# Recurrent stage of a hybrid block: reversed value tiles moved through DRAM one by one, and the heads' steps filled otherwise

## The chip, the cores and the metric

The kernel runs on one core of a Trainium2 chip. A core has a matrix engine (PE in the profile; its weight loads are PEld), VectorE (DVE), ScalarE (ACT), GpSimd (POOL) and a queue engine, SyncE (SP). Each engine works through its own instructions in order. Transfers are issued by SP, ACT or POOL and run on 16 DMA engines that all queues share. The metric is the device time of one execution in microseconds (us), the median of several runs.

## The reference

One transformer-like block on 1024 tokens of width 1024, in float32. `h` is the normalised input; `h @ w_in` gives nine projections. Three parts follow:

```python
o_hg = hgrn2_mixer(hq, hf, hi, lower_bounds[layer])      # recurrent: 8 heads, 128 keys, 128 values
o_hg = rms_norm(o_hg, hg_out_norm[layer]).reshape(b, s, HG_WIDTH) * jax.nn.sigmoid(hg)
o_sb = stick_breaking(q, k, v)                            # attention: 16 heads of 64
mixed = jax.nn.sigmoid(ga) * (o_hg @ w_hg_out) + jax.nn.sigmoid(gb) * (o_sb @ w_sb_out)
x = x + mixed @ w_o
x = x + (jax.nn.silu(gate) * up) @ w_ffn_out              # gate, up from rms_norm(x) @ w_ffn_in
```

The recurrent mixer is the part that the change touches. Its state is a 128 x 128 matrix for each head, worked out chunk by chunk (64 tokens):

```python
def step(state, inp):
    q_c, k_c, v_c, g_c = inp
    cum = jnp.cumsum(g_c, axis=-2)
    decay = jnp.exp(jnp.where(causal, cum[:, :, :, None, :] - cum[:, :, None, :, :], -jnp.inf))
    scores = jnp.einsum('bhtd,bhtsd,bhsd->bhts', q_c, decay, k_c)
    o = (jnp.einsum('bhts,bhsv->bhtv', scores, v_c)
         + jnp.einsum('bhtd,bhdv->bhtv', q_c * jnp.exp(cum), state))
    last = cum[:, :, -1:, :]
    state = (jnp.exp(last[:, :, 0, :, None]) * state
             + jnp.einsum('bhsd,bhsv->bhdv', k_c * jnp.exp(last - cum), v_c))
    return state, o
```

`q_c`, `k_c` and `g_c` come from the projections `hq` and `hf`, and the values `v_c` from the projection `hi`.

## The kernel before, in words

Every product of float32 operands is made from three matmuls (`mm3`, lines 229 to 233): each operand is split into a rounded part and a remainder (`wh`, `wl` for weights). `load_w` (from line 128) loads a block of weights with SP (`wr`), rounds it with ACT, and has POOL subtract it by an accumulating DMA (`rest_by_dma`, lines 123 to 126). Two `wr` buffers and three of `wh` and `wl` go round.

The program runs in stages: the projections of the first heads (`Pairs`, a scheme that saves products and needs sums of the quarters of `h`, the list `h_sums`), the recurrent stage, the attention stage, the output products and the feed-forward part.

In the recurrent stage the loop `for h in range(NH)` at the end of the quoted code runs over eight heads. A head has `prep` (decayed keys and queries, by POOL, ACT and DVE) and fifteen steps, the list at the end of `hg_head`: `base(0)`, `base(1)`, `across`, `level(0)` to `level(3)` (scores of pairs of ever smaller stretches, gathered in `sc`), `turn` (transposes of decayed keys, copied by ACT to `ket`, line 658), `state` (products of keys and values, line 667, joined to states by DVE), `read` (the outputs, lines 715 and 717) and `norm`. Each step works on tiles of 128 tokens; the eight tiles come in pairs `tp` = 0 to 3, the second of each pair with its tokens in reversed order.

The values `v` of heads h and h+1 come from one projection (`hg_v`, `proj_v`), four pairs of tiles for two heads together. The first tile of each pair is copied from PSUM into `v` by ACT (line 560). The second has to be reversed over the partitions, and that goes through DRAM: ACT copies it to `vs` (line 557), SP stores it to `d_v` (line 558), a DRAM-to-DRAM transfer on ACT's queue (`turn_v`, line 564) writes the rows of all four to `d_vr` in reversed order, and two transfers on ACT's queue (`load_v`, line 568) bring them to `v[:, 1::2]`. `turn_v(h)` stands at the start of `prep` of the even head h; for head 0 after its values; `load_v(h)` with `base(0)`. `state(0)` needs tiles 0 to 3 of `v`, `state(1)` tiles 4 to 6, `read(1)` also tile 7.

PE's order is exactly that of the program. `weave(own, fill, lead)` writes it: between a head's own steps it puts `fill`, other work for PE, in proportion to the numbers that the list gives each step, after `lead` units at the start. The fill of head h is the query projection of the next head (`hg_q`, 16 steps of 0.65, called q steps here), then `hg_gates` of the next head (0.0), and then half of the values of the next pair of heads (`hg_v`, 32 steps of 0.33, v steps): tiles 0 and 1 in the even heads, 2 and 3 in the odd ones. Heads 6 and 7 have gate projections in place of values. Loads, copies and other engines' instructions are ordered by a planner: it goes by the order of the program as priority and its own estimate of when each instruction can start, so one that is ready early can be put ahead of one that was written before it. Once the order is fixed, each engine and queue keeps it.

Of the kernel before, what the change touches and what calls it, by code (L numbers as in the profile page):

```python
# [16 lines left out]
P = 128  # L17
# [24 lines left out]
def hybrid_block(ctx, tc, x, norm1_gain, w_in, lb_logits, hg_out_norm, sb_q_norm, sb_k_norm,  # L42
                 w_hg_out, w_sb_out, w_o, norm2_gain, w_ffn_in, w_ffn_out,
                 c_ident, c_blk, c_lvl, c_base, out):
    nc = tc.nc
# [69 lines left out]
    d_v, d_vr = (dp.tile([NH // 2, NT // 2, P, 2 * P], F32, name=n) for n in ("d_v", "d_vr"))  # L115
# [293 lines left out]
    hd = [dict() for _ in range(NH)]  # L409
# [139 lines left out]
    def hg_v(h, tiles=range(4), get=None):  # L549
        get = get or in_block(2048 + h * P, 256)  # L550

        def evac(tp, ps):
            if tp == 0:
                for j in range(2):
                    hd[h + j]["v"] = hg.tile([P, NT, P], F32, tag="v", bufs=4, name="v")
            vs = hg.tile([P, 2 * P], F32, tag="vs", name="vs")
            nc.scalar.copy(vs, ps[:, 2 * P:])
            nc.sync.dma_start(d_v[h // 2, tp], vs)
            for j in range(2):
                nc.scalar.copy(hd[h + j]["v"][:, 2 * tp, :], ps[:, j * P:(j + 1) * P])  # L560
        return proj_v(get, evac, tiles)

    def turn_v(h):
        nc.scalar.dma_start(d_vr[h // 2], d_v[h // 2, :, ::-1, :])

    def load_v(h):
        for j in range(2):
            nc.scalar.dma_start(hd[h + j]["v"][:, 1::2, :],
                                d_vr[h // 2, :, :, j * P:(j + 1) * P].rearrange("a p c -> p a c"))

    def hg_load(h):
        d = hd[h]
# [17 lines left out]
    def hg_head(h):  # L590
        d = hd[h]
        sg, q, v, kv, c = (d[n] for n in ("sg", "q", "v", "kv", "c"))
# [2 lines left out]

        def prep():
            if h % 2 == 0 and h > 0:
                turn_v(h)
            sc = e["sc"] = hg.tile([P, S], F32, tag="sc", bufs=1, name="sc")
            nc.gpsimd.memset(sc, 0.0)  # L600
            kb = e["kb"] = hg.tile([P, S], F32, tag="kl", bufs=4, name="kb")
            qb = e["qb"] = hg.tile([P, S], F32, tag="kl", bufs=4, name="qb")
            c4 = c.rearrange("p (b l) -> p b l", l=4)
            nc.gpsimd.tensor_sub(qb.rearrange("p (b l) -> p b l", l=4), c4,
                                 c4[:, :, 1:2].broadcast_to([P, S // 4, 4]))
            for dst, src in by_tile(kb, qb):
                nc.scalar.activation(dst, src, AF.Exp, scale=-1.0)
            nc.scalar.activation(qb, qb, AF.Exp)
            order(nc.vector.tensor_mul(kb, kb, kv), *last.get("own", ()))
            nc.vector.tensor_mul(qb, qb, q)  # L610
            ke = e["ke"] = hg.tile([P, S], F32, tag="ke", bufs=1, name="ke")
            for dst, src in by_tile(ke, c):
                dst, src = (a.rearrange("p a (n c) -> p a n c", c=CH) for a in (dst, src))
                nc.gpsimd.tensor_sub(dst, src[:, :, :, CH - 1:CH].broadcast_to([P, NT // 2, 2, CH]), src)
            nc.scalar.activation(ke, ke, AF.Exp)
            order(nc.vector.tensor_mul(ke, ke, kv), *last.get("own", ()))
            el = e["el"] = hg.tile([P, 64], F32, tag="el", name="el")[:, 0:NCH]
            nc.scalar.activation(el, c3[:, :, CH - 1], AF.Exp)
            qe = e["qe"] = hg.tile([P, S], F32, tag="qe", bufs=1, name="qe")
            nc.scalar.activation(qe, c, AF.Exp)  # L620
            nc.vector.tensor_mul(qe, qe, q)

        def base(g):
            kb, qb = e["kb"], e["qb"]
            ps = pbank("pz")
            for j in range(4):
                t = 4 * g + j
                nc.tensor.matmul(ps[:, j * P:(j + 1) * P], kb[:, t * P:(t + 1) * P],
                                 qb[:, t * P:(t + 1) * P], start=True, stop=True)
            nc.vector.copy_predicated(e["sc"][:, g * HS:(g + 1) * HS], bmask, ps)  # L630

        def across():
            ke, qe, el = e["ke"], e["qe"], e["el"]
            ps = pbank("pz")
            for t in range(NT):
                r0 = t % 2 * CH
                nc.tensor.matmul(ps[r0:r0 + CH, t * CH:(t + 1) * CH], ke[:, t * P + r0:t * P + r0 + CH],
                                 qe[:, t * P + CH:(t + 1) * P], start=True, stop=True)
            for w, rows in enumerate((slice(0, CH), slice(CH, P))):
                nc.scalar.copy(pairs(e["sc"])[rows, :, w, CH:], ps[rows, :].rearrange(  # L640
                    "p (a two c) -> p a two c", two=2, c=CH)[:, :, w, :])
            el2 = el.rearrange("p (t two) -> p t two", two=2)
            nc.vector.tensor_mul(chunk0(ke), chunk0(ke), el2[:, :, 1:2].rearrange("p (a two) o -> p a two o", two=2)
                                 .broadcast_to([P, NT // 2, 2, CH]))
            nc.vector.tensor_mul(bl(qe, CH)[:, :, 1, :], bl(qe, CH)[:, :, 1, :],
                                 el2[:, :, 0:1].broadcast_to([P, NT, CH]))
            eb = e["eb"] = hg.tile([P, 64], F32, tag="eb", name="eb")[:, 0:NT]
            nc.vector.tensor_mul(eb, el2[:, :, 0], el2[:, :, 1])
# [28 lines left out]
        def level_prep(li):  # L677
            L = LEVELS[li]
            kq = hg.tile([P, 2, HS], F32, tag="kl", bufs=4, name="kq")
            kp, qr = kq[:, 0, :], kq[:, 1, :].rearrange("p (b l) -> p b l", l=L)  # L680
            halves = [a.rearrange("p a (b two l) -> p a b two l", two=2, l=L)[:, :, :, 0, :]
                      for k3 in [kp.rearrange("p (a x) -> p a x", x=P)] for a in (k3, odd(k3))]
            cl = bl(c, L)
            for w, dst in enumerate(halves):
                src = pairs(c)[:, :, w, :].rearrange("p a (b two l) -> p a b two l", two=2, l=L)[:, :, :, 0, :]
                nc.vector.tensor_sub(dst, src[:, :, :, L - 1:L].broadcast_to([P, NT // 2, P // (2 * L), L]), src)
            nc.gpsimd.tensor_sub(qr, cl[:, :, 1, :], cl[:, :, 0, L - 1:L].broadcast_to([P, HS // L, L]))
            nc.scalar.activation(kq, kq, AF.Exp)
            nc.vector.tensor_mul(qr, qr, bl(q, L)[:, :, 1, :])
            k4 = kp.rearrange("p (a b two l) -> p a b two l", two=2, l=L, a=NT // 2)  # L690
            for w in range(2):
                nc.vector.tensor_mul(k4[:, :, :, w, :], k4[:, :, :, w, :], pairs(kv)[:, :, w, :].rearrange(
                    "p a (b two l) -> p a b two l", two=2, l=L)[:, :, :, w, :])
            e[li] = kq
# [27 lines left out]
        def norm(half):  # L722
# [7 lines left out]
            nc.sync.dma_start(d_ohg[h][:, sl], r)  # L730

        return prep, [
            (0.86, lambda: (base(0), load_v(h) if h % 2 == 0 else None, level_prep(0),)),
            (2.46, lambda: (base(1), level_prep(1),)),
            (5.60, lambda: (across(), level_prep(2),)),
            (2.24, lambda: (level(0), level_prep(3),)),
            (0.50, lambda: (turn(0),)),
            (0.80, lambda: (turn(1),)),
            (0.85, lambda: (level(1),)),
            (1.85, lambda: (state(0),)),  # L740
            (0.70, lambda: (state(1),)),
            (0.61, lambda: (level(2),)),
            (3.99, lambda: (level(3),)),
            (1.60, lambda: (read(0),)),
            (4.50, lambda: (read(1),)),
            (2.97, lambda: (norm(0),)),
            (0.45, lambda: (norm(1),)),
# [54 lines left out]
    for n in range(n0):  # L802
        if n == n0 - 5:
            get = in_block(2048, 256)
            get()
            v0 = [hg_v(0, tiles, get) for tiles in ((0, 1), (2, 3))]
        weave([], pairs0.steps(n))
        if h_sums:
            h_sums.pop(0)()
    s0ctx.close()  # L810
    hg = hgctx.enter_context(tc.tile_pool(name="hg", bufs=2, reuse_waits="tile"))
# [4 lines left out]
    prep, own = hg_head(0)  # L816
    prep()
    weave([], v0[1])
    turn_v(0)
    def urgent(steps):  # L820
        def run(f):
            with tc.high_priority():
# [3 lines left out]
    for h in range(NH):  # L826
        if h < NH - 1:
            fill = hg_q(h + 1) + [(0.0, lambda: hg_gates(h + 1))]
            if h == NH - 2:
                fill += gate_steps(1)  # L830
            if h < NH - 2:
                fill += hg_v(h + 1, (2, 3)) if h % 2 else hg_v(h + 2, (0, 1))
        else:
            fill = gate_steps(2)
        load_blocks()
        if h > 0:
            prep, own = hg_head(h)
            prep()
        if h < NH - 1:
            hg_load(h + 1)  # L840
        weave(own, fill, lead=5.53)
    hgctx.close()


# [686 lines left out]
```

## Time and profile before

| | |
|---|---|
| median of 3 runs | 2054.48 us (2050.78 to 2055.08) |
| the profiled execution | 2053.37 us; span from first to last instruction 2051.3 us |
| PE, DVE, ACT, POOL busy | 98%, 74%, 56%, 16% of the span |
| mean granted PE clock | 0.993 |
| `d_vr<-d_v` (ACT queue) | 4 issues of 512 KB |
| `v<-d_vr` (ACT queue) | 8 issues of 256 KB, 2.8 us to landing |
| `d_v<-vs` (SP queue) | 16 issues of 128 KB, 1.7 us to landing |

How to read it: a row of a group or a timeline names the line of the kernel, the engine, the operation, `out<-in` by the names of the program, the shape and the count; square brackets hold the idle time of the engine just before it and what ended it. A row of waits reads "engine, tile, line <- who released it: us in total, times, longest". A busy PE is not PE at its peak, since matmuls overlap and a low clock makes them longer.

### The profile page before, as it was taken

The numbers are of one execution on the slowest core, as the hardware profiler recorded it, in microseconds if no ns is written. First come the engines' busy times: TensorE is split into PE (matmuls) and PEld (weight loads), VectorE is DVE, ScalarE is ACT, GpSimd is POOL, SyncE is SP. The second block draws the span as 40 slices with busy tenths as digits, with TensorE's granted clock in tenths as the row PEclk, the third lists the DMA queues.
The fourth block names the chain that finished last, engine by engine and source line by source line (L and its number), as shares of the span: only waits on it lengthen the run. The fifth ranks groups of instructions, "written<-read, shape, count | busy, mean of one in ns | idle before, by whom it ended". The sixth has DMA issues, their size and how long they took to land.

```text
span 2051.3 us, 29673 instructions
## 1 busy us (share of the span) xinstructions
PE 2006.9 (98%) x10963; PEld 1720.6 (84%) x10963; DVE 1522.5 (74%) x2355; ACT 1141.7 (56%) x1957; POOL 318.4 (16%) x431
## 2 busy tenths in 40 slices
PE   8999899999999999999999999998999999999999
PEld 8888788898888988988988888887888888888887
DVE  7853777787367877787787598999766666668975
ACT  7544464555377777777777465547433333334443
POOL 0000444444222332332231000000000000000000
PEclk9999999999999999999999999999999999999999
DMA  5234446545455445455445646413323222256131
GB/s 184 98 114 144 128 120 158 144 114 152 117 117 125 89 107 118 99 118 121 101 105 120 216 147 210 166 35 111 102 74 105 78 72 77 78 203 222 42 113 41
DMA packets 209840, 245.23 MB, mean 120 GB/s; under 512 B 12008, under 2 KB 142496, under 8 KB 209696
## 3 DMA queue, kind: packets, MB, share of 16 engines
q1 hardware_dynamic: 188928, 202.84, 31.4%
q0 software_dynamic: 13616, 35.14, 10.3%
q10 hardware_dynamic: 7152, 5.37, 0.8%
q8 instruction: 86, 1.41, 0.3%
q14 instruction: 58, 0.48, 0.1%
HBM read 146.57 MB, written 51.12 MB: 96 GB/s over the span
## 4 chain that ended last, share of the span: by engine, by line
PE 71%; DVE 9%; DMA 4%; issue 2%; ACT 2%; POOL 1%; DVEq 0%; POOLq 0%; ACTq 0%
PE pd L231 14%; PE pd L232 14%; PE pd L233 14%; DMA d_vr<-d_v 3%; PE pt L1011 3%; PE pt L233 3%; PE pt L231 3%; PE pt L232 3%; PE po L1028 2%; PE po L231 2%; PE po L1027 2%; PE po L232 2%; PE po L233 2%; PE pz L966 2%; PE pz L967 2%
## 5 line engine op out<-in xcount | busy, mean ns | idle before, releaser
L167 ACT CAST wh<-u 128x512 fp32r<-128x512 f32 (+1 forms) x280 | 183.5, 684 | 224.9 <-PE po L233 86.6
L231 PE MATMUL pd<-hT,wh 128*128 128x512 f32 (+1 forms) x716 | 286.7, 400 | 0.0
L232 PE MATMUL pd<-hT,wh 128*128 128x512 f32 (+1 forms) x716 | 276.0, 385 | 0.5 <-DVE hT L281 0.5
L233 PE MATMUL pd<-hT,wl 128*128 128x512 f32 (+1 forms) x688 | 264.9, 385 | 0.0
L231 PE MATMUL pd<-u,wh 128*128 128x512 f32 x496 | 194.0, 391 | 1.5 <-ACT c L1394 0.7
L232 PE MATMUL pd<-u,wh 128*128 128x512 f32 x496 | 193.1, 389 | 0.2 <-DVE u L168 0.2
L168 DVE TENSOR_TENSOR wl<-u,wh 128x512 fp32r<-128x512 f32 (+1 forms) x196 | 150.5, 801 | 45.7 <-ACT wh L167 43.6
L231 PE MATMUL pd<-wh,hT 128*128 128x256 f32 x512 | 153.6, 300 | 0.0
L233 PEld LDWEIGHTS pd<-hT,wl 128*128 128x128 f32 x688 | 129.2, 188 | 26.9
L978 DVE TENSOR_TENSOR_SCAN kp<-kp,dsel 128x512 f32<-128x512 f32 (+3 forms) x128 | 123.5, 965 | 37.0 <-ACT kp L971 36.4
L232 PEld LDWEIGHTS pd<-hT,wh 128*128 128x128 f32 x716 | 135.2, 189 | 18.7 <-DVE hT L281 0.9
L231 PEld LDWEIGHTS pd<-hT,wh 128*128 128x128 f32 x716 | 135.0, 189 | 18.2
L232 PE MATMUL pd<-wl,hT 128*128 128x256 f32 x512 | 145.7, 285 | 2.7 <-DMA wl<-wr 1.7
L233 PE MATMUL pd<-wh,hT 128*128 128x256 f32 x512 | 145.6, 284 | 0.0
L971 ACT ACTIVATE kp<-pz,rq 128x128 f32<-128x128 f32 (+2 forms) x192 | 114.2, 595 | 43.9 <-PE pz L967 33.2
L233 PE MATMUL pd<-u,wh 128*128 128x512 f32 x352 | 137.0, 389 | 0.0
L164 DVE TENSOR_TENSOR u<-u,u 128x512 f32<-128x512 f32 (+1 forms) x152 | 124.7, 855 | 12.3 <-DMA u<-d_ohg 7.6
L1014 DVE TENSOR_TENSOR tl<-pt,th 128x512 fp32r<-128x512 f32 (+1 forms) x160 | 100.2, 627 | 33.5 <-ACT th L1013 33.1
L985 DVE TENSOR_TENSOR a<-a,kp 128x128 f32<-128x128 f32 (+2 forms) x192 | 109.7, 571 | 17.8 <-ACT a L971 3.4
L971 ACT ACTIVATE a<-pz,rq 128x128 f32<-128x128 f32 (+2 forms) x192 | 114.3, 595 | 7.0 <-PE pt L1011 7.0
L231 PEld LDWEIGHTS pd<-u,wh 128*128 128x128 f32 x496 | 93.1, 188 | 21.6 <-ACT c L1394 1.1
L232 PEld LDWEIGHTS pd<-u,wh 128*128 128x128 f32 x496 | 93.1, 188 | 19.8 <-DVE u L168 0.5
(305 smaller groups left out, 5293.5 us busy)
## 6 DMA issues: line engine op xcount, KB each, us to landing
wr<-in_w_in SPq DMA_DIRECT2D x72, 512.0 KB, 4.0
wl<-wr POOLq DMA_DIRECT2D x59, 512.0 KB, 4.9
u<-in_w_ffn_in SPq DMA_DIRECT2D x24, 512.0 KB, 4.7
wr<-in_w_ffn_in SPq DMA_DIRECT2D x20, 512.0 KB, 4.2
u<-in_w_ffn_out SPq DMA_DIRECT2D x10, 1024.0 KB, 6.7
d_act<-c SPq DMA_DIRECT2D x33, 256.0 KB, 2.1
u<-d_act SPq DMA_DIRECT2D x8, 1024.0 KB, 5.7
qh<-qh SPq DMA_DIRECT2D x48, 128.0 KB, 2.4
```

Source lines behind the costliest of these rows:

```text
L164: e.tensor_tensor(raw(to), raw(a), raw(b), op=op)
L167: nc.scalar.copy(hi, src)
L168: e.tensor_sub(lo, src, hi.bitcast(F32))
L231: nc.tensor.matmul(ps, lh, rh, start=start, stop=False, skip_group_check=adds)
L232: nc.tensor.matmul(ps, lh, rl, start=False, stop=False, skip_group_check=adds)
L233: nc.tensor.matmul(ps, ll, rh, start=False, stop=stop, skip_group_check=adds)
L966: nc.tensor.matmul(ps[:, :n], qhi[:, qs], kk[:, k0:k0 + n], start=True, stop=False)
L971: last["sig"] = [nc.scalar.activation(t[:, 0:w], ps[:, 0:w], AF.Sigmoid, scale=rq[:, n_, col:col + 1]) for n_, t in enumerate((kp, a))]
L978: nc.vector.tensor_tensor_scan(rev, rev, dsel[:, HS - w:][:, ::-1], initial=0.0, op0=ALU.mult, op1=ALU.max)
L985: nc.vector.tensor_mul(a[:, 0:w], a[:, 0:w], kp[:, 1:w + 1])
L1011: nc.tensor.transpose(tp[:, s * P:(s + 1) * P], a[:, b * P:(b + 1) * P], ident)
L1014: nc.vector.tensor_sub(tl[:, c0:], tp[:, c0:], th[:, c0:].bitcast(F32))
```

## The change

- `turn_v(h, tp)` now moves one tile of a pair of heads: 128 rows in reversed order, each as two runs of 128 numbers, with the two heads as the outer dimension. It is issued by ACT. Tiles 0 to 2 are moved after the store of the tile behind them (`tp > 0` in `evac`), tile 3 with the step `base(1)` of the even head.
- `load_v(h, tiles)` is issued by SP: tiles 0 to 2 at the start of `prep` of the even head (for head 0 after its values), tile 3 with `level(1)`.
- The numbers of the steps for `weave` are others, and `lead` is 3.64 instead of 5.53.
- In the first stage the remaining `h_sums` begin after the third step of `pairs0` instead of the first.

```diff
@@ hg_v, evac
             nc.sync.dma_start(d_v[h // 2, tp], vs)
+            if tp > 0:
+                turn_v(h, tp - 1)
@@
-    def turn_v(h):
-        nc.scalar.dma_start(d_vr[h // 2], d_v[h // 2, :, ::-1, :])
-
-    def load_v(h):
+    def turn_v(h, tp):
+        dst, src = (d[h // 2, tp].rearrange("p (j c) -> j p c", j=2) for d in (d_vr, d_v))
+        nc.scalar.dma_start(dst, src[:, ::-1, :])
+
+    def load_v(h, tiles):
         for j in range(2):
-            nc.scalar.dma_start(hd[h + j]["v"][:, 1::2, :],
-                                d_vr[h // 2, :, :, j * P:(j + 1) * P].rearrange("a p c -> p a c"))
+            nc.sync.dma_start(hd[h + j]["v"][:, 1 + 2 * tiles.start:2 * tiles.stop:2, :],
+                                d_vr[h // 2, tiles, :, j * P:(j + 1) * P].rearrange("a p c -> p a c"))
@@ prep
             if h % 2 == 0 and h > 0:
-                turn_v(h)
+                load_v(h, slice(0, 3))
@@ hg_head, the list of steps
-            (0.86, lambda: (base(0), load_v(h) if h % 2 == 0 else None, level_prep(0),)),
-            (2.46, lambda: (base(1), level_prep(1),)),
-            (5.60, lambda: (across(), level_prep(2),)),
+            (1.53, lambda: (base(0), level_prep(0))),
+            (2.70, lambda: (base(1), turn_v(h, 3) if h % 2 == 0 else None, level_prep(1),)),
+            (3.27, lambda: (across(), level_prep(2),)),
             (2.24, lambda: (level(0), level_prep(3),)),
-            (0.50, lambda: (turn(0),)),
-            (0.80, lambda: (turn(1),)),
-            (0.85, lambda: (level(1),)),
-            (1.85, lambda: (state(0),)),
-            (0.70, lambda: (state(1),)),
+            (0.35, lambda: (turn(0),)),
+            (0.49, lambda: (turn(1),)),
+            (0.85, lambda: (level(1), load_v(h, slice(3, 4)) if h % 2 == 0 else None,)),
+            (1.79, lambda: (state(0),)),
+            (0.60, lambda: (state(1),)),
             (0.61, lambda: (level(2),)),
-            (3.99, lambda: (level(3),)),
-            (1.60, lambda: (read(0),)),
+            (11.14, lambda: (level(3),)),
+            (0.47, lambda: (read(0),)),
             (4.50, lambda: (read(1),)),
             (2.97, lambda: (norm(0),)),
             (0.45, lambda: (norm(1),)),
@@ first stage
-        if h_sums:
+        if h_sums and n > 1:
             h_sums.pop(0)()
@@ before the loop over the heads
-    turn_v(0)
+    load_v(0, slice(0, 3))
@@ the loop
-        weave(own, fill, lead=5.53)
+        weave(own, fill, lead=3.64)
```

## The prediction, made before the result was known

> **What bounds the kernel now.** I read the page first (span and busy time), then the busy time by stretch, one stretch for each head of the recurrent stage, then what the matrix engine (PE) waited for, and last the chain of waits and the DMA queues round those waits.
>
> ```profile
> span 2051.3 us, 29673 instructions
> ...
> PE 2006.9 (98%) x10963; PEld 1720.6 (84%) x10963; DVE 1522.5 (74%) x2355; ACT 1141.7 (56%) x1957; POOL 318.4 (16%) x431
> ```
>
> PE sets the end nearly everywhere, so an edit pays only where PE idles or runs slowly. The stretches below are heads 0 to 4 (start and end of a head are where its first fill step runs). The columns are stretch, length, then busy time and count of PE, PEld, DVE, ACT, POOL, the granted PE clock, the DMA share and GB/s.
>
> ```profile
> 217.90:266.50 48.60, 38.34 (x266) 34.93 (x265) 34.68 (x52) 23.20 (x36) 13.51 (x14) 0.89 0.45 117
> 266.50:303.50 37.00, 35.94 (x265) 32.82 (x264) 28.86 (x51) 22.13 (x36) 18.71 (x15) 1.00 0.53 136
> 303.50:345.70 42.20, 37.81 (x266) 34.43 (x265) 31.28 (x45) 22.59 (x37) 16.38 (x15) 0.96 0.53 144
> 345.70:382.50 36.80, 35.74 (x264) 32.63 (x263) 28.62 (x50) 21.89 (x35) 18.67 (x15) 1.00 0.53 136
> 382.50:426.00 43.50, 39.16 (x265) 35.80 (x264) 31.24 (x45) 22.54 (x37) 16.36 (x15) 0.92 0.51 140
> ```
>
> Odd heads take 37 us, even ones 42 to 49, with the same PE instructions. Two things differ: idle time, and PE busy time at a lower clock (35.84 on average in heads 1 and 3 against 38.34, 37.81 and 39.16, so 2.50 + 1.97 + 3.32 = 7.8 us lost to the clock). The idle time of the whole stage (195 to 560 us), by cause:
>
> ```profile
> PE pt L667 <- ACT ket L658: 13.8, 5, 8.4
> PE pt L667 <- DMA v<-d_vr: 3.3, 4, 1.0
> PE pt L715 <- DVE sc L703: 2.5, 3, 1.1
> PE pd L232 <- DMA wl<-wr: 1.7, 2, 0.9
> PE pz L390 <- DVE sql L385: 1.3, 3, 0.4
> PE pd L232 <- ACT kq L688: 1.0, 1, 1.0
> ```
>
> The first two groups are the `state(0)` matmuls of the even heads, in the timeline of PE:
>
> ```profile
> 246.28 0.80 PE L667 MATMUL pt<-v,ket 128*128 128x128 f32 x2 [8.39 <-ACT ket L658]
> 247.54 0.80 PE L667 MATMUL pt<-v,ket 128*128 128x128 f32 x2 [0.46 <-DMA v<-d_vr]
> ...
> 325.39 0.49 PE L667 MATMUL pt<-v,ket 128*128 128x128 f32 x2 [2.07 <-ACT ket L658]
> 326.89 1.65 PE L667 MATMUL pt<-v,ket 128*128 128x128 f32 x6 [1.01 <-DMA v<-d_vr]
> ...
> 404.39 0.49 PE L667 MATMUL pt<-v,ket 128*128 128x128 f32 x2 [2.13 <-ACT ket L658]
> 405.85 1.44 PE L667 MATMUL pt<-v,ket 128*128 128x128 f32 x5 [0.98 <-DMA v<-d_vr]
> ...
> 481.84 0.49 PE L667 MATMUL pt<-v,ket 128*128 128x128 f32 x2 [0.63 <-ACT ket L658]
> 483.14 0.94 PE L667 MATMUL pt<-v,ket 128*128 128x128 f32 x6 [0.81 <-DMA v<-d_vr]
> ```
>
> That is 8.85 + 3.08 + 3.11 + 1.44 = 16.5 us. The chain of waits of head 2 and ScalarE's timeline there say why:
>
> ```profile
> 303.74 0.26 ACT vs L557
> ...
> 305.81 17.95 DMA d_vr<-d_v
> ...
> 323.78 3.07 DMA v<-d_vr
> ```
> ```profile
> 324.75 0.97 ACT L658 COPY ket<-pt 128x512 f32<-128x512 f32 x2 [7.48 <-DMA d_vr<-d_v]
> ```
>
> The turn through DRAM begins when the last of four tiles has been stored, takes 17.95 us, and its loads (3.07 us) stand in ScalarE's own queue: ScalarE idles 7.48 us in front of them, and its next copy, `ket`, feeds the same matmuls.
>
> **The tile moves and loads.** The rows of the DMA queues: the turn of head 2 and then its loads (share of 16 engines in stretches of 17.9 and 3.5 us), the store of one tile, the weight remainders that run beside the turn, and SP's queue.
>
> ```profile
> q10 hardware_dynamic: 516, 0.52, 9.0%
> wl<-wr POOLq DMA_DIRECT2D x2, 512.0 KB, 11.6
> ```
> ```profile
> q10 hardware_dynamic: 1056, 0.52, 51.6%
> ```
> ```profile
> d_v<-vs SPq DMA_DIRECT2D x16, 128.0 KB, 1.7
> ```
> ```profile
> 217.57 0.32 SPq L558 DMA_DIRECT2D d_v<-vs  x1
> ...
> 290.07 0.37 SPq L136 DMA_DIRECT2D wr<-in_w_in  x1
> 292.25 12.12 SPq L558 DMA_DIRECT2D d_v<-vs  x2
> 305.99 2.97 SPq L730 DMA_DIRECT2D d_ohg<-r  x2
> 309.01 0.77 SPq L575 DMA_DIRECT2D sg<-d_g  x1
> 317.04 4.51 SPq L136 DMA_DIRECT2D wr<-in_w_in  x2
> ```
>
> The old turn is 512 packets of 1 KB and 4 more; 9.0% of 16 engines over 17.9 us is 25.8 us, 50 ns a packet. I read the 4 as one completion per engine used: 128 packets on each of four engines, 6.4 us of work stretched to 17.95 by the other queues. The loads come out the same way at 27 ns a packet of 512 B, on all 16 engines.
>
> The new move of one tile is 256 packets of 512 B. No row shows it. Its lower bound is the 128 KB store, 1.7 us; its upper bound the whole old turn, 17.95. I take 8: 128 packets at 50 ns on each of two engines, 6.4, and 1.7 to begin and land.
>
> The Trainium skill (DMA: Bandwidth & Descriptors, section "Why a DMA increments its semaphore by 16 and not by 1") says that a copy runs on the largest number of engines up to 16 that divides the outermost dimension of both sides; the 4 extra packets of the old turn, with four tiles outermost, agree. By it the new form, with the two halves outermost, gets two engines, which speaks against the change.
>
> When is the third tile, the last that `state` needs, in place? Its source is stored at 292.25 (the first of the two), landed 1.7 later. Queue orders come from the planner, which lets a ready transfer pass: the weights that PE uses from 303.5 on were issued by 290.07, though the program names them at head 2. So the move should be issued between 294.0 and, if it stays behind the copy `vs` of tile 3, 304.0. With 8 for the move and 3.07 for the load, `v` lands between 305.1 and 315.1.
>
> When does PE want it? The fill list of an even head is 16 q steps (0.65 each) and 32 v steps (0.33), 20.96. `weave` pumps it to lead + (20.96 - lead) x done/sum. After `level(1)` that was 5.53 + 15.43 x 13.31/29.98 = 12.38 (16 q, 7 v) and becomes 3.64 + 17.32 x 11.43/33.96 = 9.47 (15 q). Two PE rows of head 2 price a step, and two more rows set head 0 and the `h_sums` edit:
>
> ```profile
> 313.53 0.69 PE L637 MATMUL pz<-qe,ke 128*64 128x64 f32 x16
> 317.00 1.05 PE L702 MATMUL pz<-kq 128*128 128x128 f32 x8
> ```
> ```profile
> 227.17 0.36 ACT L557 COPY vs<-pd 128x256 f32<-128x256 f32 x1
> ```
> ```profile
> 76.77 0.50 PE L231 MATMUL pd<-hi,wh 128*128 128x512 f32 x1 [1.21 <-ACT c L516]
> ```
>
> Four q steps lie between the first two: (317.00 - 313.53 - 0.69)/4 = 0.70 us each; a v step has half the columns, 0.35. So `state(0)` comes 0.70 + 7 x 0.35 = 3.2 us earlier. In head 2 it was due at 325.39 - 2.07 = 323.3, of which 0.9 was the wait for `wl` before it; it will be due at 319.2. The loads have landed 4 to 14 us before. Heads 4 and 6 repeat this, so heads 2, 4 and 6 lose 3.08 + 3.11 + 1.44 us of idle time, and the slow clock, whose stretches in the table all follow these waits, goes with it: 7.8.
>
> Head 0 is tighter. Its `state(0)` was due at 246.28 - 8.39 = 237.9, and will be at 237.9 - 1.0 (the wait for `kq`) - 3.2 = 233.7. Tile 2 is stored at 217.57. If its move passes ScalarE's late `vs` of tile 3 (227.17), `v` lands at 217.6 + 1.7 + 8 + 3.1 = 230.4; behind it, at 227.5 + 8 + 3.1 = 238.6, 4.9 late. I take a mean of some 2.5 and 0.5 of slow clock: 3 us of the saving lost.
>
> **The turns issued by ScalarE, the loads by SP.** Per pair of heads ScalarE issued one turn (0.6) and two loads (0.9 us) and will issue four moves; it is busy 22 of 37 us, and that idle time hides them. If the cover were gone: four at SP's 0.32 are no more than the 1.5 before. What matters is that ScalarE's wait for the turn (7.48) moves to SP. Queued behind SP's waits are the gate load (`sg`, 309.01) and the weights at 317.04, which PE wants in the next head, at 345.7; 28.7 us less 11.6 for the remainder leaves some 15 us of slack after the load itself. The fourth tile's move follows the third's by about 8 us and is wanted only by `read(1)`, in the last third of the head.
>
> The Trainium skill (DMA: Bandwidth & Descriptors, section "Issuing engines are not separate DMA queues") says that changing the issuing engine saves only issue time. By it the part would be worth nothing; the 7.48 us that ScalarE spends waiting is not issue time, so the trace disagrees in effect.
>
> **Filling placed otherwise.** By the same `weave` sums, v steps start after `state(0)` instead of before it, and the q steps lie earlier. The `wl` and `kq` waits (1.7 + 1.0) stand at an early v step, now 2 to 3 us later in the head: gone. Between `level(3)` and `read(0)` there were 7 v steps (2.5 us) and will be 18 (6.3), so the 2.5 of waiting for `sc`, 1.1 at the longest, goes. Against that, `base(0)` to `level(3)` all come 2 to 3 us earlier after the head's start while VectorE (29 to 31 us a head) has to prepare them. Nothing shows what that costs; the nearest rows are the waits for VectorE, 0.4 and 1.1. With none to 1.1 in each of seven heads: 0 to 7.7. I take 0.4 each, 3 in all, since VectorE will still have 5 us a head to spare.
>
> **`h_sums` from the third step.** The only wait in its stretch is the 1.21 above, for a ScalarE copy. Bounds by that row: 1.2 gained to 1.2 lost; I take 0, since the last sums are wanted after 76.77 and VectorE's work is the same.
>
> **Sum.** 16.5 (late `v`) + 7.8 (clock) + 2.7 (`wl`, `kq`) + 2.5 (`sc`) = 29.5; less 3 (head 0) and 3 (new waits): 23.5. The profiled execution took 2053.4 us, 2.1 more than its span; 2053.4 - 23.5 = 2029.9. It lies 1.1 below the median of 2054.5; between the two bases I forecast **2031**. With all 29.5 and the 1.2: 2053.4 - 30.7 = 2022.7, so 2023. With 4.9 late in head 0 and 7.7 of new waits: 2053.4 - 29.5 + 5.5 + 7.7 = 2037.
>
> **The rivals.**
>
> *VectorE becomes the bound.* At 36 us a head it is 80 to 87% busy, and everything from `base(1)` to `level(3)` has 1.2 us less room (8.4 to 20.4 us after the head's start becomes 6.4 to 17.2 for `level(2)`, by the `weave` order with these steps). For it: waits for `sc` and `sql` already stand in the trace. Against: in head 3 VectorE was idle 8 us. Price: up to twice 1.1 in each of seven heads, 15: 2029.9 + 15 - 3 = 2042.
>
> *The moves are no quicker than the old turn.* One tile then takes 17.95 us, since two engines carry as many packets each as four did. If moves also stay behind `vs`, `v` lands at 304.0 + 17.95 + 3.07 = 325.0 in head 2, where it was 326.9; 1.9 x 3 is gained there, nothing in head 0, and the clock stays low. With `sc` (2.5) that is 8: 2045. The skill's rule on the number of engines, above, is what would bring it about. Against: it needs both the slow move and the bad order; the stretch of the old turn was made by queues that the new moves, at 294, run before.
>
> *Slower: SP stands behind the moves.* Third and fourth tile share their engines. If the two together take over 28 us from 304.0 (317.0 + 15 = 332), the load of the fourth holds SP so long that the next head's weights are late. At 2 x 17.95 it is 339.9, 8 us late in heads 1, 3 and 5, some 24 and half as much of slow clock: 2045 + 36 = 2081. It decides only from 28 us on; my value gives 16.
>
> *No change.* The queues may be ordered so that ScalarE still waits, now for the tile stores, as long as it did: 2054.
>
> **How the numbers follow.** Forecast 0.60, VectorE 0.17, slow moves 0.10, SP 0.07, no change 0.06. The likeliest case's own range is 2023 to 2037; adding most of the second and third gives **2023 to 2046**, with some 0.8. Within 0.2% (4 us) is what a measurement of this kernel can't tell from no change. Faster: 0.60 + 0.17 + 0.10 = 0.87; same 0.06; slower 0.07.
>
> **What would show it.** Right: even heads of 36 to 38 us at clock 1.00, no PE wait at L667 over 1 us but in head 0, no wait of ScalarE for `d_vr`, the wait for `sc` gone. Wrong: PE waits at L667 for `v` over 3 us after head 0 (slow moves), PE waits at L702 for `kq` or at L637 (VectorE), or waits for `wl` early in odd heads with SP waiting for `d_vr` (SP).

## The result and the profile after

The changed kernel takes 2035.1 us (median, 2034.7 to 2037.1) against 2053.9 for the kernel before on the same chip: a ratio of 0.9913 with a 95% interval of 0.9896 to 0.993. Beside later experiments, on another chip, it took 2033.4 against 2056.1: 0.9884 (0.9867 to 0.99). The profiled execution took 2035.3 us.

The first view is the page's head (span, busy time):

```profile
span 2033.5 us, 29691 instructions
...
PE 2003.3 (99%) x10963; PEld 1716.7 (84%) x10963; DVE 1522.2 (75%) x2355; ACT 1144.1 (56%) x1957; POOL 316.8 (16%) x431
```

17.8 us of span have gone, 3.6 of them from PE's busy time (the clock), the rest from its idle time. The waits of PE in the recurrent stage (190 to 545 us: total, times, longest) are now:

```profile
PE pz L389 <- ACT sqh L384: 5.9, 3, 4.8
PE pd L231 <- DVE q L425: 1.5, 1, 1.5
PE pz L390 <- DVE sql L385: 0.9, 4, 0.2
PE pt L670 <- ACT ket L661: 0.7, 2, 0.4
PE pz L705 <- DVE kq L695: 0.5, 1, 0.5
```

(Lines behind the diff stand 3 lower: L667 is L670 now, L658 L661.) The waits for `v`, `sc` and `wl` are gone and that for `ket` is down to 0.7: 23.6 us of idle time have become 9.5. But half of what is left, 4.8, is one wait that the kernel before did not have. It lies in head 0, as the stretches of heads 0, 1, 2 and 4 show (columns as in the prediction):

```profile
218.69:264.19 45.50, 38.73 (x266) 34.72 (x265) 35.71 (x56) 27.32 (x42) 17.59 (x16) 0.93 0.48 123
264.19:301.47 37.28, 36.07 (x264) 32.75 (x263) 28.87 (x46) 20.67 (x32) 14.53 (x14) 1.00 0.53 138
301.47:338.57 37.10, 36.34 (x264) 32.68 (x263) 30.68 (x47) 22.20 (x36) 16.38 (x15) 1.00 0.59 157
...
375.58:412.17 36.59, 36.12 (x265) 32.77 (x264) 30.37 (x47) 22.41 (x36) 16.75 (x15) 1.00 0.61 159
```

The later even heads are like the odd ones now, 36 to 37 us at full clock. Head 0 is not: 45.5 us, of 48.6 before, at clock 0.93. Measured from `base(0)` to the next head's `base(0)`, heads 0 to 6 gained 3.1, -0.3, 4.9, 0.0, 6.7, 1.4 and 2.0 us; `base(0)` of head 0 comes 1.25 earlier and the last head takes 2.0 longer. Together that is 17.1 of the 17.8.

What holds head 0 is seen in PE's timeline there, then in the chain of waits, and then in ScalarE's:

```profile
258.73 0.79 PE L389 MATMUL pz<-sqh,ones 128*128 128x512 f32 x1 [4.82 <-ACT sqh L384]
```
```profile
248.18 1.57 POOL kv L588
249.74 0.02 issue
249.76 0.32 SPq L578
250.08 0.05 issue
250.13 6.32 DMA d_v<-vs
256.45 0.02 issue
256.47 0.57 ACTq L567
257.04 0.05 issue
257.08 1.08 ACT o L722 x2
258.17 0.52 ACT sqh L384
```
```profile
246.65 0.37 ACT L557 COPY vs<-pd 128x256 f32<-128x256 f32 x1
...
256.47 0.57 ACTq L567 DMA_DIRECT2D d_vr<-d_v  x1
257.08 1.08 ACT L722 ACTIVATE o<-pt 128x512 f32<-128x512 f32 x2 [3.87 <-DMA d_v<-vs]
```

Read the chain backwards. `norm(0)` waits for `sqh`, which ScalarE makes from `o` (L722). ScalarE could have made `o` 3.87 us earlier, but ahead of it in its queue stands a move (L567), here of tile 0 of the values of heads 2 and 3, which head 0's fill projects. The move waits for its tile's store (L558). The tile was copied to `vs` by 247.0, but SP issued the store only at 250.13, behind a load of a gate (L578) that waited for GpSimd's `kv`. The store then took 6.32 us. Before, 1.7 was the median, but the trace gives the landing of only three of the 16 stores; four other stores that a move waits for in the changed kernel took 3.2 to 4.3. SP's timeline shows what went out just ahead of the slow one, two loads of 512 KB:

```profile
248.67 0.38 SPq L136 DMA_DIRECT2D wr<-in_w_in  x1
249.76 0.32 SPq L578 DMA_DIRECT2D fv<-d_f  x1
```

### The profile page after: what moved, and what is told of

It is laid out like the page before. It is cut to its first block, busy times and chain, and to the rows that moved or that the text cites. A ratio compares the mean times of both kernels' runs of the same rounds, so it can differ in the third digit from the quotient of the medians.

```text
span 2033.5 us, 29691 instructions
## 1 busy us (share of the span) xinstructions
PE 2003.3 (99%) x10963; PEld 1716.7 (84%) x10963; DVE 1522.2 (75%) x2355; ACT 1144.1 (56%) x1957; POOL 316.8 (16%) x431
## 4 chain that ended last, share of the span: by engine, by line
PE 70%; DVE 13%; issue 2%; ACT 2%; DMA 2%; POOL 1%; ACTq 0%; DVEq 0%; SPq 0%; POOLq 0%
PE pd L231 14%; PE pd L232 14%; PE pd L233 14%; PE pt L1014 3%; PE pt L231 3%; PE pt L233 3%; PE pt L232 3%; DVE u L164 2%; PE po L1031 2%; DVE u L168 2%; PE po L231 2%; PE po L1030 2%; PE po L233 2%; PE po L232 2%; PE pz L969 2%
## 5 line engine op out<-in xcount | busy, mean ns | idle before, releaser
L232 PEld LDWEIGHTS pd<-hT,wh 128*128 128x128 f32 x716 | 135.7, 190 | 17.8 <-DVE hT L281 0.7
L988 DVE TENSOR_TENSOR a<-a,kp 128x128 f32<-128x128 f32 (+2 forms) x192 | 109.4, 570 | 18.1 <-ACT a L974 3.3
L231 PEld LDWEIGHTS pd<-u,wh 128*128 128x128 f32 x496 | 93.1, 188 | 21.4 <-ACT c L1397 1.1
L1016 ACT CAST th<-pt 128x512 fp32r<-128x512 f32 (+1 forms) x160 | 87.5, 547 | 39.5 <-PE pt L1014 29.2
```

The costliest lines, as they stand in the source:

```text
L231: nc.tensor.matmul(ps, lh, rh, start=start, stop=False, skip_group_check=adds)
L232: nc.tensor.matmul(ps, lh, rl, start=False, stop=False, skip_group_check=adds)
L988: nc.vector.tensor_mul(a[:, 0:w], a[:, 0:w], kp[:, 1:w + 1])
L1016: nc.scalar.copy(th[:, c0:], tp[:, c0:])
```

## The experiments

**The two halves apart.** The kernel before with the new path of the values alone, the step numbers and the lead as they were:

```diff
+            if tp > 0:
+                turn_v(h, tp - 1)
...
-        nc.scalar.dma_start(d_vr[h // 2], d_v[h // 2, :, ::-1, :])
+        dst, src = (d[h // 2, tp].rearrange("p (j c) -> j p c", j=2) for d in (d_vr, d_v))
+        nc.scalar.dma_start(dst, src[:, ::-1, :])
...
-            nc.scalar.dma_start(hd[h + j]["v"][:, 1::2, :],
+            nc.sync.dma_start(hd[h + j]["v"][:, 1 + 2 * tiles.start:2 * tiles.stop:2, :],
```

> The kernel before with the new way of the values alone (moves by tile on ScalarE's queue, loads on SP); the numbers of the steps, the lead and h_sums as before. If the late values were the cost (16.5 us idle and 7.8 us of slow clock), most of the gain is here: 2054 less 16 to 24, so 2030 to 2038, with no wait at the state matmuls over 1 us in heads 2, 4 and 6. If the filling carries the gain, 2048 or more.

And the kernel before with the new numbers alone:

```diff
-            (5.60, lambda: (across(), level_prep(2),)),
+            (3.27, lambda: (across(), level_prep(2),)),
...
-            (3.99, lambda: (level(3),)),
+            (11.14, lambda: (level(3),)),
...
-        weave(own, fill, lead=5.53)
+        weave(own, fill, lead=3.64)
```

> The kernel before with the new numbers of the steps and the new lead alone; the values still turned in one piece and loaded on ScalarE's queue. If the landing of the values sets the even heads, state(0) stands 3.2 us earlier on PE and waits that much longer in four heads (+12.8), while the waits for sc (2.5) and for wl and kq (2.7) go: 2054 + 8 = 2062. If the filling carries the gain: 2036 to 2045.

The path alone took 2039.6 against 2056.8: 0.992 (0.9905 to 0.9935). Most of the gain is here, though the time lies just above the 2030 to 2038 that were expected. The filling alone took 2066.1, which is slower: 1.0049 (1.0034 to 1.0064), and by more than the 2062 that were expected. Two rows of PE's waits for the first kernel, and one for the second, say why:

```profile
PE pt L718 <- DVE sc L706: 7.6, 7, 3.4
PE pz L705 <- DVE kq L695: 4.6, 3, 2.1
```
```profile
PE pt L667 <- ACT ket L658: 31.5, 7, 11.0
```

With the path alone `state` waits no more, but the waits for `sc` grow from 2.5 to 7.6: they move to the next place where the old filling is thin. With the filling alone the waits for `sc` at L715, for `wl` and for `kq` do go, but `state` comes earlier and waits for the old turn the longer, 31.5 us where it was 13.8. So the two are not a sum: by itself the filling costs some 9 us; on top of the path it is worth a few at most (0.9884 to 0.9913 for both, 0.992 for the path). These were not run side by side, and the intervals of 0.9913 and 0.992 overlap, so the size of that part is not shown.

**`h_sums` from the third step**, alone in the kernel before:

```diff
-        if h_sums:
+        if h_sums and n > 1:
```

> The kernel before with h_sums begun after the third step alone. By the prediction no change: 2053 to 2055. The wait of 1.2 us for ScalarE's copy in that stretch bounds a gain; the trace after shows two such waits of 1.4 in all where there were 1.9.

2057.6 against 2056.8, a ratio of 1.0003 (0.9994 to 1.0013): nothing, as the prediction's sum had it.

**The issuing engine.** The kernel before with its one turn, and only the loads of `v` moved to SP; and the changed kernel with its loads moved back to ScalarE:

```diff
-            nc.scalar.dma_start(hd[h + j]["v"][:, 1::2, :],
+            nc.sync.dma_start(hd[h + j]["v"][:, 1::2, :],
```

> The kernel before with the two loads of v on SP's queue in place of ScalarE's, still one turn of four tiles. If the landing of the turn is the cost, the wait moves from ScalarE to SP and PE still stands at state(0) until v lands: 2050 to 2056. If ScalarE's idle time before the loads (7 to 10 us in the even heads) is the cost: the ket wait of 13.8 us goes, 2040 or less.

```diff
-            nc.sync.dma_start(hd[h + j]["v"][:, 1 + 2 * tiles.start:2 * tiles.stop:2, :],
+            nc.scalar.dma_start(hd[h + j]["v"][:, 1 + 2 * tiles.start:2 * tiles.stop:2, :],
```

> The changed kernel, with the loads of v on ScalarE's queue again. If what counts is that the turn begins early, tile by tile, the loads find their moves landed and the issuer makes little difference: 2034 to 2038. If SP as issuer is what frees ScalarE (it stood 7.5 to 10 us in front of the loads before), ScalarE stands again and ket is late: 2040 to 2050, with waits at the state matmuls for ket.

The first took 2056.7, a ratio of 1.0 (0.9991 to 1.001); the second 2034.6, 0.9901 (0.9885 to 0.9918), like the changed kernel itself. PE's largest wait in the first:

```profile
PE pt L667 <- DMA v<-d_vr: 18.0, 4, 9.9
```

ScalarE's copy of `ket` no longer stands behind the loads, and PE waits at the same matmuls for `v` itself, 18.0 us where it was 17.1 for `ket` and `v` together. ScalarE's wait for the turn only covered that wait. The engine that issues the loads is worth nothing here in either kernel. The Trainium skill (DMA: Bandwidth & Descriptors, section "Issuing engines are not separate DMA queues") says that starting transfers from several engines saves only the time of starting them. The prediction held that the trace disagreed in effect; these two runs agree with the rule.

**The moves begun late.** The changed kernel with the moves of tiles 0 to 2 held behind ScalarE's copy of tile 3:

```diff
-            if tp > 0:
-                turn_v(h, tp - 1)
+            if tp == 3:
+                for t in range(3):
+                    order(turn_v(h, t), done)
```

> The changed kernel, with the moves of tiles 0 to 2 held behind ScalarE's copy of tile 3, so that all of them start late, at once. The planner may order other work round it otherwise. If the gain comes from the early start of the moves: ScalarE's and the matrix engine's waits for the values return in the even heads (over 2 us a head at state(0) or at the copies in front of it, heads 2, 4, 6 over 40 us), time over 2044. Rival (the gain comes from the moves being small and quick, at most 5 us each, with the loads off ScalarE's path): three moves take at most 15 us from about 304 in head 2, the values land by 322, wanted at about 319 to 320, heads 2, 4 and 6 lose under 3 us each, and the time is under 2044.

2053.4 against 2056.1: 0.9991 (0.9981 to 1.0002). The whole gain is gone, though the moves are as small as before. Three rows of PE's waits, one of ScalarE's, and ScalarE's timeline round the moves in head 2:

```profile
PE pt L671 <- DMA v<-d_vr: 12.0, 4, 5.2
PE pz L706 <- ACT sc L644: 6.0, 1, 6.0
PE pt L671 <- ACT ket L662: 5.3, 3, 1.8
```
```profile
ACT v L563 <- issue: 22.5, 4, 6.9
```
```profile
305.80 0.59 ACTq L568 DMA_DIRECT2D d_vr<-d_v  x1
306.07 0.36 ACT L557 COPY vs<-pd 128x256 f32<-128x256 f32 x1
306.42 5.32 ACTq L568 DMA_DIRECT2D d_vr<-d_v  x2
311.78 0.43 ACT L563 COPY v<-pd 128x128 f32<-128x128 f32 x2 [5.35 <-issue]
```

The direct wait in heads 2, 4 and 6 is 2.5, 2.0 and 2.4, which fits both expectations (2 or more, under 3); in head 2 three moves are done 12.8 us after the first issue (SP issues the loads at 318.62), as the rival had it. But the time and the length of these heads (40.2, 39.6 and 40.0 us) are those of the first: issued close together, the moves hold ScalarE for 5 to 7 us at their issue in each even head, and in head 0 `sc`, queued behind them, holds PE for 6.0 us. The waits for `ket` stand in the odd heads, 1.8 in each. So small moves alone are not enough: by this run they need the early start, for the data and for the engine that issues them. A caution belongs to this run and to the next: the added edge made the planner order much else otherwise as well, so the size of the loss is not that of the edge alone.

**The new wait in head 0.** First, each move put behind ScalarE's `vs` copy of the next tile, so that ScalarE can't stand before a store so early:

```diff
-                turn_v(h, tp - 1)
+                order(turn_v(h, tp - 1), done)
```

> The changed kernel, with each move of a tile (tiles 0 to 2) held behind ScalarE's copy vs of the following tile by an edge on ScalarE's own queue; same work, same queues. If the 4.8 us wait at norm(0) of head 0 and the slow clock behind it (2.6) come from ScalarE standing at the move of tile 0 until its store has landed (256.5), both go: 2035 less 5 to 8, so 2027 to 2030, and head 0 takes 37 to 40 us instead of 45.5. If ScalarE is late there for its own work, no change: 2035, with the wait still at L389.

Head 0 took 41.5 us (37 to 40 expected) and the wait was gone, yet the kernel took 2048.1 against 2056.0, 0.9965 (0.9955 to 0.9975): slower than the changed kernel. Its PE waits:

```profile
PE pz L705 <- DVE kq L695: 11.3, 8, 2.6
PE pz L390 <- DVE sql L385: 3.8, 3, 1.3
```

The planner's new order had VectorE prepare `kq` late, and heads 2 and 4 took 41.6 and 42.0 us. Then the stores issued by ScalarE instead of SP, which leaves the moves where they are:

```diff
-            nc.sync.dma_start(d_v[h // 2, tp], vs)
+            nc.scalar.dma_start(d_v[h // 2, tp], vs)
```

> The changed kernel, with the stores of vs to d_v issued by ScalarE instead of SP. In head 0 the store stood on SP behind a gate load that waited for GpSimd, was issued 3.1 us after its copy and then took 6.3 us behind 1 MB of loads. If that delay is the cause, ScalarE no longer waits at the move of tile 0 and the 4.8 + 2.6 us go: 2027 to 2030. If ScalarE's wait is only for the landing itself, at least 2 us of waiting stay in each of 16 places on ScalarE: 2033 to 2037.

2033.4, 0.9895 (0.988 to 0.9909); head 0 takes 41.6 us, but the time is in the range of the second expectation. Because the ratio looked better than that of the changed kernel, both were run side by side on one chip in five rounds, with a third that moves the stores of `h == 0` alone:

```diff
-            nc.sync.dma_start(d_v[h // 2, tp], vs)
+            (nc.scalar if h == 0 else nc.sync).dma_start(d_v[h // 2, tp], vs)
```

> The changed kernel once more, beside the others of this series: ratio 0.990 to 0.992 to the kernel before, 2035 us.

> The changed kernel with all stores of the value tiles issued by ScalarE, beside the changed kernel itself. If the store behind SP's loads is the cause of the lost time in head 0: 2 to 4 us (0.1 to 0.2%) below the changed kernel. Rival (no difference): within 1 us of it.

> The changed kernel, with the stores of the value tiles issued by ScalarE in head 0 alone (four stores; the matrix engine's order stays the same). If the 4.8 us wait of norm(0) in head 0 comes only from the store of a tile standing behind loads on SP's queue: head 0 takes about 41.5 us as it did with all stores moved, some 4 us less than the 45.5 of the changed kernel, the other heads stay at 34.7 to 37.3, time 4 us below the changed kernel's, about 2031. Rival (head 0 is slow because the stage's first head runs with a cold clock and late preparation, whatever the store does): head 0 stays within 1 us of 45.5 and the time within 1 us of the changed kernel's.

| kernel | median, us | ratio to before |
|---|---|---|
| changed kernel | 2033.36 (2033.13 to 2033.9) | 0.9884 (0.9867 to 0.99) |
| all stores by ScalarE | 2033.24 (2032.61 to 2034.47) | 0.9884 (0.9869 to 0.9899) |
| stores of `h == 0` by ScalarE | 2033.84 (2032.61 to 2037.25) | 0.9889 (0.9874 to 0.9904) |

The stretches of head 0 and head 2, first of the changed kernel in this series and then with all stores by ScalarE:

```profile
222.49:267.74 45.25, 38.54 (x264) 34.60 (x263) 33.98 (x55) 28.53 (x42) 18.62 (x16) 0.92 0.55 137
...
305.13:342.06 36.93, 36.27 (x264) 32.69 (x263) 30.72 (x48) 22.23 (x36) 16.37 (x15) 1.00 0.57 147
```
```profile
221.38:262.23 40.85, 37.65 (x264) 33.83 (x264) 32.97 (x53) 25.85 (x40) 17.74 (x15) 0.96 0.57 142
...
299.98:337.56 37.58, 36.35 (x264) 32.69 (x264) 31.01 (x47) 22.29 (x36) 16.50 (x15) 1.00 0.56 146
```

Two rows of PE's waits in the second (190 to 545 us):

```profile
PE pt L670 <- ACT ket L661: 3.1, 5, 0.7
PE pz L390 <- DVE sql L385: 2.6, 5, 1.7
```

The cause of the wait is shown: with the store off SP's queue the wait of `norm(0)` in head 0 falls from 4.7 us, for ScalarE's `sqh`, to 1.7, now for VectorE's `sql` in the matmul behind it, and the head is 4.4 us shorter. But no time is gained: the medians are 0.1 us apart, as the rival had it. Heads 1 to 5 take 0.3 to 0.8 us more each, 2.5 in all; 2.0 of that are waits for `ket` (3.1 us in all, 1.1 in the changed kernel). The attention stage starts 2.9 us earlier, and 1.5 of that is lost again behind it, in a place that no run here isolates. The third kernel misses its target: the store that blocks is of the values of heads 2 and 3, and `h` is 2 there. Its SP queue is unchanged at that place, `norm(0)` still waits 3.4 us, and head 0 takes 44.1. It says nothing on the cause. No variant that was run beats the changed kernel.

**Four engines for a move.** The last dimension cut in four, not in two:

```diff
-        dst, src = (d[h // 2, tp].rearrange("p (j c) -> j p c", j=2) for d in (d_vr, d_v))
+        dst, src = (d[h // 2, tp].rearrange("p (j c) -> j p c", j=4) for d in (d_vr, d_v))
```

> The changed kernel, with each move cut in four runs of 64 numbers a row instead of two of 128, with the four outermost: by completions it should run on four engines instead of two, with 128 packets of 256 B each. If the bytes per engine set a move's time, it lands in some 60% of the 5.1 us that lie at most between its issue and its load; if packets per engine or the start and landing do, it does not get shorter. The kernel's time stays at 2035 in both cases, since no PE wait stands at the moves of heads 2, 4 and 6; 2040 or more if shorter packets slow the weights beside them.

2034.9, 0.9903 (0.9883 to 0.9923): no difference. The queue of the moves in 5.6 us that hold one move of head 2 and no other transfer of that queue (packets, MB, share of 16 engines), in the changed kernel and in this one:

```profile
q10 hardware_dynamic: 258, 0.13, 7.7%
```
```profile
q10 hardware_dynamic: 516, 0.13, 10.3%
```

256 packets of 512 B and 2 completions become 512 of 256 B and 4. The busy time is 0.077 x 16 x 5.6 = 6.9 us or 27 ns a packet on two engines, and 9.2 us or 18 ns a packet on four. From the issue of the move to that of the load it takes 5.1 us and then 4.1. One microsecond less on a move that is done some 15 us before its values are wanted (next section) changes nothing. The counts of completions agree with what the Trainium skill (DMA: Bandwidth & Descriptors, section "Why a DMA increments its semaphore by 16 and not by 1") says of the number of engines.

## Why the prediction was right, and where it was not

The forecast was 2031; the runs gave 2035.1 and 2033.4, both faster, in the range. The sum had 23.5 us; the profiled execution became 18.1 shorter, and the shortfall is about what head 0 missed. By its own steps:

**Heads 2, 4 and 6: right.** The sum had 3.08, 3.11 and 1.44 us of waiting and, in heads 2 and 4, 1.97 and 3.32 of slow clock; these heads gained 4.9, 6.7 and 2.0, and their granted clock is 1.00. In head 2 ScalarE's queue has the order that gives the prediction's early bound, the move ahead of `vs` of tile 3 (302.64), in the timelines of the two queues:

```profile
296.56 0.57 ACTq L567 DMA_DIRECT2D d_vr<-d_v  x1
```
```profile
292.28 0.32 SPq L558 DMA_DIRECT2D d_v<-vs  x1
301.67 0.90 SPq L571 DMA_DIRECT2D v<-d_vr  x2
```
```profile
317.48 1.16 PE L670 MATMUL pt<-v,ket 128*128 128x128 f32 x8 [0.38 <-ACT ket L661]
```

The store took 4.3 us where the prediction had 1.7, so the move was issued at 296.56 (forecast 294 to 304). The loads came 5.1 us later, so that `v` is there some 12 us before `state(0)` wants it at 317.1. That is 15.6 us after the start of the head; the prediction had 319.2 - 303.5 = 15.7.

**A tile's move, 8 us: too long.** It takes 5.1. The term that was mis-sized is the price of a packet: 50 ns was that of 1 KB, and one of 512 B takes 27, as in the prediction's own row of the loads: 128 x 27 ns + 1.7 = 5.2. It did not matter, since the start of the moves decides, as the late moves show. The rival of slow moves is out by the same number.

**Head 0, "3 us of the saving lost": wrong, and the largest miss.** That step weighed only whether `v` would be late, and it was not: `vs` of tile 3, which the step had at 227.17, was copied at 218.90, the loads were issued at 225.80, and `state(0)` at 236.67 waits for nothing. But a move on ScalarE's queue can do two things, bring `v` late or hold up ScalarE, and the step looked at the first alone. With 8.85 us for the late `v`, 2.5 of clock, 1.0 of `kq` and 3 lost, head 0 should have gained 9.4; it gained 3.1. The missing 6 us went to `norm(0)` standing behind a move that waits for its store (4.8), to a wait of 1.5 for VectorE's `q`, and to a clock of 0.93 as low as in a head with a stall. The mechanism stood among the rivals, in the one of no change (ScalarE waits for the tile stores instead), with a chance of 0.06 and as all or nothing. In truth it occurs in most heads and bites in one. ScalarE's waits for stores (195 to 530 us):

```profile
ACT sqh L384 <- DMA d_v<-vs: 8.1, 4, 2.7
ACT o L722 <- DMA d_v<-vs: 3.9, 1, 3.9
ACT v L562 <- DMA d_v<-vs: 1.9, 1, 1.9
```

13.9 us of waiting, of which only the 3.9 in head 0 stalls PE at length. The wait is a real cost of the change; the side-by-side runs also say that taking it away in the way tried is worth nothing: other waits grow, and part is lost in a place not isolated.

**"What matters is that ScalarE's wait for the turn (7.48) moves to SP": wrong.** Moving the loads alone gave a ratio of 1.0, and moving them back one of 0.9901, no other than the whole change. PE wanted `v` itself at the same place. SP does wait in front of the loads now, 31.8 us in five places, 9.0 at the longest, in head 2, and PE does not wait for what is behind it: it has no wait for `wl` left in the stage. The rival of SP standing behind the moves is out.

**The filling, 2.7 + 2.5: right for the waits, not shown in the time.** The waits for `wl` and `sc` are gone and that for `kq` has halved to 0.5. But heads 1 and 3, where `sc` was waited for 1.1 us each, gained -0.3 and 0.0, and alone the filling costs some 9 us; what it is worth on top of the path these runs don't settle. New waits were set at 3; beside the one in head 0, PE waits 4.7 in all, of which 2.6 are new (1.1 for `sqh`, 1.5 for `q`). VectorE has not become the bound in this kernel; with another order of its queue it can (11.3 us for `kq` in the run with the moves behind the copies). `h_sums`: 0 forecast, 0 measured.

## What to carry to other kernels

Before a wait is moved to another queue, ask whether the engine that matters wants the data at that place anyway; if it does, only an earlier start of the transfer helps. A transfer that waits for another transfer holds all that stands behind it on the engine that issues it, so price each such issue by its worst case (a store behind large loads, 6.3 us where others took 1.7 to 4.3), head by head, and not for all heads at once. A filling that was tuned for one set of due times can cost time with another: measure the parts of such a change together as well as apart.

## What the runs showed of the hardware

A 128 KB store issued right behind 1 MB of loads on the same queue took 6.3 us; four others of the changed kernel took 3.2 to 4.3, three of the kernel before 1.7. A DRAM-to-DRAM packet took 18, 27 and 50 ns for 256 B, 512 B and 1 KB, the first two with hardly another transfer in that time, the last beside 2.9 MB of others.

Moves of 256 packets on two engines (by their two completions), issued in quick succession by ScalarE, held ScalarE at the issue: in the timeline above the first of three took 0.59 us and the other two 5.3 together. Two issued 0.9 us apart at the start of head 0 of the changed kernel took 0.57 and 1.18. What limits them was not tried.

An idle time of the same size can cost clock or not. In the run with late moves, head 2 has a wait of 2.5 us and head 4 one of 2.0:

```profile
310.08:350.30 40.22, 36.25 (x265) 32.77 (x264) 34.28 (x48) 26.25 (x42) 17.68 (x17) 1.00 0.58 150
...
387.58:427.15 39.57, 37.40 (x265) 34.15 (x264) 32.91 (x48) 26.23 (x42) 21.56 (x17) 0.96 0.59 152
```

The longer wait left the clock at 1.00; in the head with the shorter one it was 0.96, and PE was busy 1.15 us longer with the same 265 matmuls. The Trainium skill (TensorE: Matmul & The Clock Gate, "Part 1: The HAM clock gate") says that activity is judged over a window of some 3.4 us that runs freely, and that the clock falls after an idle window. A window that runs freely could make like stalls count differently, but a stall of 2.0 us fills no window of 3.4: there the measurement differs from the Trainium skill, and what lets the clock fall here stays open.
